# One core of attention: two instruction streams mixed by weights, with order edges between them added, other weights, and scales formed at other places

## The chip, the cores and the metric

The kernel runs on one core of a Trainium2 chip. The metric is the device time of one execution in microseconds. The engines are TensorE (PE; its weight loads, PEld, are listed apart), VectorE (DVE), ScalarE (ACT), GpSimd (POOL) and SyncE (SP), which issues nearly all DMA here. Each engine works through its own queue of instructions in the order in which the compiled program put them.

## What is computed

One inference step of a decoder of two layers, for a prompt of 2048 tokens and, beside it, 8 samples of 4 tokens each (1024 wide). Layer 0 has four heads of a gated linear recurrence (HGRN2) and four heads of forgetting attention; layer 1 is gated linear attention (GLA). The samples' attention reads its 2048 past keys and values from pages of a cache by a page table. The change touches the attention:

```python
def fox_prompt(q, k, v, log_f):                      # 16 blocks of 128 queries, 4 heads of 128
    c = jnp.cumsum(log_f, axis=1).swapaxes(1, 2)
    ...
    logits = einsum('bthd,bshd->bhts', qi, k) * scale + ci[..., None] - c[:, :, None, :]
    logits = jnp.where(t[:, None] >= key_pos[None, :], logits, -jnp.inf)
    p = jax.nn.softmax(logits, axis=-1)
    return einsum('bhts,bshd->bthd', p, v)

def fox_sample(q, k, v, log_f, k_pages, v_pages, logf_pages, page_table):   # 8 samples, 4 tokens
    k_past = k_pages[page_table].reshape(db, -1, H, dh)      # 16 pages of 128 rows a sample
    v_past = v_pages[page_table].reshape(db, -1, H, dh)
    ...
    p = jax.nn.softmax(concatenate([logit_past, logit_new], axis=-1), axis=-1)
    return einsum('bhts,bshd->bthd', p[..., :P], v_past) + einsum('bhts,bshd->bthd', p[..., P:], v)
```

The rest of a layer (the projections before, the output projection after) is matmul of 1024-wide weights.

## The kernel before, in words

The program has three phases: the projections of layer 0 with HGRN2 in two halves of 1024 tokens, then attention (`phase_fox`, from L1099), then the output of layer 0 and all of layer 1. Operands of matmuls that must be exact are held as two f16 parts (`h_*` and `l_*`, or `th` and `tl`), and `mm3` (L452 to L454) does three f16 matmuls for one product. To fit f16 the operands are scaled by powers of two; the scales are columns of one small tile `kc`, given out by `kcol` (L237).

**Two streams.** Attention is written as two Python generators, mixed by `mux` (L72). Each `yield` hands over a cost; `mux` takes the next piece of whichever stream has the smaller share of its total so far, and the totals are the constants `FOX_P` and `FOX_S`. The costs that the sample's stream hands over are constants too: `SC_C` for one head of one turn of keys, `PV_C` for one set of values. The mixing order is the order of tracing. A scheduler then places the instructions on each engine by it, by priority, and by extra edges: `issue_after(x)` says that what is traced inside stands behind `x` on the engine of `x`. Nothing of it is decided while the program runs; at run time engines only wait for data and for buffers.

**The prompt's stream** (`fox_prompt`, L1139) goes through 16 groups (head h, group G of 512 queries). `loads(h, G)` brings queries, keys, bias, values and the gate (`raw_q`, `raw_k`, `cb`, `raw_v`, `fsg`) by SyncE, and splits them: ACT writes `h_*`, POOL `l_*`; for values ACT first multiplies by the scale `self.sv`. It is called in the middle of the group before. `scores` makes one row of 128 queries: `s` on TensorE (`mm3`), the softmax on DVE, ACT and POOL (`mx`, `nm`, tiles `L`). `values` makes the output: TensorE transposes `L` to `pt` (L1217), ACT rounds `pt` to `th` (L1224), DVE takes the remainder `tl` (L1225), and `mm3` adds into `fo`.

**The sample's stream** (`fox_sample`, L1282) first goes through 32 turns of keys: four pages (`pgcache_fox_k`, 256 KB each) are fetched, TensorE transposes them into `pkt` (L1331), ACT and DVE copy them to `kts` (two copies each a turn, L1334 and L1335), and four `strips` of matmuls that lie side by side in the array add scores into `sc`. After turn 3 `past` sums the forget values of the cache. Then comes the softmax, and then the values: two accumulators `pv0` and `pv1`, each of 16 sets of four pages `pgcache_fox_v` and one set of new values; a set is four strips (L1465), one page each, with `high_priority`. Pages share one pool of `PG` = 27 buffers of 256 KB. SyncE issues every page (L1302) after it has loaded the page's number from the table into a register, four numbers at a time.

**Scales.** `y_bounds` (L1505), called at the start of `phase_fox`, forms bounds of the outputs of both layers, with three matmuls `spr_gh`, `spr_vm`, `spr_gg` (L248) that spread a maximum over the partitions and a chain of small DVE operations on single columns. It also forms `self.sv`, the scale of the prompt's values, from `vmax`, the measured maximum of the values (taken tile by tile in the projections). For queries and keys, `fox_scale` (L1487) does it from a bound that is known when the projection starts.

Of the kernel before, what the change touches and what calls it, by code (L numbers as in the profile page):

```python
# [8 lines left out]
F32 = mybir.dt.float32  # L9
# [6 lines left out]
ALU = mybir.AluOpType  # L16
# [3 lines left out]
P = 128  # L20
# [7 lines left out]
NPG = 16  # L28
# [5 lines left out]
S0 = 12000.0  # L34
SC_C = 700.0
Z_C = 4000.0
# [11 lines left out]
PG = 27  # L48
PAST = 12
NG = 2  # L50
WSPLIT = 4
FOX_S = 335000.0
FOX_P = 270000.0
# [5 lines left out]
DEC = 4500.0  # L59
PV_C = 4600.0  # L60
NEG = -1e30
# [41 lines left out]
class Kern:  # L103
# [6 lines left out]
    def consts(self):  # L110
        nc, i = self.nc, self.i
# [15 lines left out]

        self.kc, self.n_kc, self.scales = cp.tile([P, 176], F32, name="kc"), 0, {}
        self.vmax = cp.tile([P, NPG], F32, name="vmax")
# [107 lines left out]
    def kcol(self, n=1):  # L237
        self.n_kc += n
        assert self.n_kc <= 176
        return self.kc[:, self.n_kc - n : self.n_kc]  # L240
# [209 lines left out]
    def mm3(self, ps, lh, rh, first, last):  # L450
        nc = self.nc
        nc.tensor.matmul(ps, lh[0], rh[0], start=first, stop=False)  # L452
        nc.tensor.matmul(ps, lh[0], rh[1], start=False, stop=False)  # L453
        nc.tensor.matmul(ps, lh[1], rh[0], start=False, stop=last)  # L454

# [310 lines left out]
    def even_half(self, hf, act, wpool, wp, pps, npool, S):  # L766
# [94 lines left out]
        def mk_bkv(hp, which):  # L861
# [3 lines left out]
            def run(W):  # L865
                cs = slice(hp * 256, hp * 256 + 256)
                held = []
                if which == "k" and hf == 0:
                    self.fox_scale("k", hp)

# [65 lines left out]
    def phase_even(self):  # L936
# [4 lines left out]
        with pool("act", side="right") as ap, pool("w", side="right") as w0, pool("wl", side="right") as wp1, \  # L941
# [5 lines left out]
            nrm = Pool(n0, {"th": 1, "nss": 4, "rs_t": 4, "rs_r": 4})  # L947
            self.scales2, self.ready, self.fsc, self.logit = {}, {}, {}, {}
            self.sx_even = self.gain_scale(self.g_even, pps, "pj", "e")
# [155 lines left out]
    def phase_fox(self):  # L1105
        tc, nc = self.tc, self.nc
        with tc.tile_pool(name="fe", bufs=2, reuse_waits="tile") as f1, \
# [8 lines left out]
            nc.gpsimd.affine_select(caus, caus, [[-1, P]], ALU.is_ge, FAR, base=0, channel_multiplier=1)  # L1116
            self.y_bounds(pps)
            with tc.tile_pool(name="fs", bufs=1, side="right", reuse_waits="tile") as s0:
# [20 lines left out]
    def fox_prompt(self, fx, pps, caus):  # L1139
# [3 lines left out]
        self.turns = []  # L1143
        self.sample_done = False

# [6 lines left out]

        def loads(h, G):
            gs = slice(G * 512, (G + 1) * 512)
            Q[h, G] = self.load_split(fx, self.qTd[h][:, gs], f"q{h}{G}", "q")
            K[h, G] = self.load_split(fx, self.kTd[h][:, gs], f"k{h}{G}", "k")
            bias(h, G)
            vsrc = self.vd[gs, h * P : (h + 1) * P].rearrange("(c s) d -> s c d", s=P)
            V[h, G] = self.load_split(fx, vsrc, f"v{h}{G}", "v", self.sv[:, 0:1])
            SG[h, G] = fx.tile([P, 512], F32, tag="sg", name=f"fsg{h}{G}")  # L1160
            nc.sync.dma_start(SG[h, G], self.sgd[h][:, gs])

        def scores(h, G, b):
# [36 lines left out]
        def values(h, G, rows, po, b1, b2):  # L1200
# [29 lines left out]
            for j in range(nj):  # L1230
                if j + len(ahead) < nj:
                    ahead.append(turn(j + len(ahead)))
                th, tl, parts = ahead.pop(0)
                for s, a, c0 in parts:
                    vv = [x[:, (s % 4) * P : (s % 4 + 1) * P] for x in V[h, s // 4]]
                    self.mm3(po[:, c0:c2], vv, [x[:, a : a + c2 - c0] for x in (th, tl)], s == 0, s == ns - 1)
                yield sum(c2 - c0 for _, _, c0 in parts) * 2.1
            y = fx.tile([P, 512], F32, tag="y", name=f"fy{h}{G}{b1}")
            nc.vector.scalar_tensor_tensor(y[:, c1:c2], po[:, c1:c2], self.sv[:, 2:3], SG[h, G][:, c1:c2], ALU.mult,
                                           ALU.mult)  # L1240
# [23 lines left out]
    def strips(self, makers, sources):  # L1264


        with self.tc.high_priority():
# [4 lines left out]
            for m in makers[1:]:  # L1272
                m()

    def fox_sample(self, fs, pps):
# [29 lines left out]

        yield S0

        qs = one([P, NH, TS], "qs")
# [85 lines left out]
        for n in range(4 * DB + 1):  # L1394
            if n < 4 * DB:
# [57 lines left out]
        for g in range(2):  # L1453
            pv = pps.tile([P, 512], F32, tag="sc", name=f"pv{g}")
            for j in range(NPG + 1):
                makers, sources = [], []
                for bb in range(4):
# [5 lines left out]
                    else:  # L1463
# [23 lines left out]
    def fox_scale(self, which, hp):  # L1487


        nc = self.nc  # L1490
        c = self.scales[f"B{which}{hp}"][:, 2:3]
        up, down = self.fsc[which, hp] = self.kcol(), self.kcol()
        nc.vector.tensor_scalar(down, c, 2.0**19, 2.0**-20, ALU.mult, ALU.max)
        if which == "q":
            nc.vector.tensor_scalar(up, c, 2.0**20, 2.0**-19, ALU.mult, ALU.min)
            nc.vector.tensor_scalar(up, up, SCALE, None, ALU.mult)
            return
        nc.vector.reciprocal(up, down)

        ib, beta = self.logit[hp] = self.kcol(), self.kcol()  # L1500
# [3 lines left out]
    def y_bounds(self, pps):  # L1504
# [394 lines left out]
```

## Time and profile before

| | |
|---|---|
| median of 3 runs | 2440.97 us (2440.67 to 2441.5) |
| profiled execution, own time | 2450.02 us |
| its span | 2448.3 us, 54207 instructions |
| busy in the span | PE 2325.6 (95%), PEld 1652.6 (67%), DVE 1464.5 (60%), ACT 1131.8 (46%), POOL 746.5 (30%) |
| moved | 316.96 MB, mean 129 GB/s |
| pages of keys and of values | 128 and 128, 256.0 KB each, 3.9 and 3.7 us from issue to landing |

The profile is one execution, so its times are set against its own 2450.02 us, not against the median of the runs. Engine rows give busy time; what an engine waited for stands in brackets behind an instruction, or in the list of waits as "engine tile line <- releaser: us in total, times, longest". A busy TensorE may be running at a lower granted clock, which shows as a longer time of the same instruction. In the list of groups, f16 matmuls of the projections cost the most (L452 to L454, 282.5, 282.6 and 282.3 us for the output projection alone); of attention, the prompt's transposes L1217 take 89.5 us (x544), the page transposes L1331 78.3 us (x512). Attention is the 15th to 22nd of the page's forty slices, where the DMA moves 199 to 255 GB/s.

### The profile page before, as it was taken

The numbers are of one execution on the slowest core, as the hardware profiler recorded it, in microseconds if no ns is written. First come the engines' busy times: TensorE is split into PE (matmuls) and PEld (weight loads), VectorE is DVE, ScalarE is ACT, GpSimd is POOL, SyncE is SP. The second block draws the span as 40 slices with busy tenths as digits, with TensorE's granted clock in tenths as the row PEclk, the third lists the DMA queues.
The fourth block names the chain that finished last, engine by engine and source line by source line (L and its number), as shares of the span: only waits on it lengthen the run. The fifth ranks groups of instructions, "written<-read, shape, count | busy, mean of one in ns | idle before, by whom it ended". The sixth has DMA issues, their size and how long they took to land. (4 is left out here: it accounts for less than half of the span.)

```text
span 2448.3 us, 54207 instructions
## 1 busy us (share of the span) xinstructions
PE 2325.6 (95%) x21116; PEld 1652.6 (67%) x21116; DVE 1464.5 (60%) x3337; ACT 1131.8 (46%) x2465; POOL 746.5 (30%) x825
## 2 busy tenths in 40 slices
PE   7999999999999989999788999999999999998998
PEld 5667668855655865666345786777768766666887
DVE  7656657446765637667556353665675555557564
ACT  6433343343433137666456454545542645545243
POOL 2223323012213235533333320332443222322233
PEclk9999999999999989999999999999999999999999
DMA  6222235435431277666684631222246312114454
GB/s 178 77 80 70 75 105 170 142 106 147 140 114 58 89 233 232 222 199 202 217 255 134 214 107 44 62 74 75 66 140 191 116 45 62 43 57 151 141 194 151
DMA packets 297955, 316.96 MB, mean 129 GB/s; under 512 B 39729, under 2 KB 241010, under 8 KB 297698
## 3 DMA queue, kind: packets, MB, share of 16 engines
q1 hardware_dynamic: 295234, 308.98, 40.0%
q8 instruction: 166, 2.72, 0.5%
q10 hardware_dynamic: 2160, 3.93, 0.4%
q14 instruction: 91, 0.75, 0.1%
q0 software_dynamic: 304, 0.59, 0.1%
HBM read 242.31 MB, written 71.11 MB: 128 GB/s over the span
## 5 line engine op out<-in xcount | busy, mean ns | idle before, releaser
L452 PE MATMUL pt_o<-w_o,act 128*128 128x256 f16 x1024 | 282.5, 276 | 2.7 <-ACT w_o L334 1.4
L453 PE MATMUL pt_o<-w_o,act 128*128 128x256 f16 x1024 | 282.6, 276 | 0.9 <-POOL w_o L335 0.9
L454 PE MATMUL pt_o<-w_o,act 128*128 128x256 f16 x1024 | 282.3, 276 | 0.0
L452 PEld LDWEIGHTS <-act 128*128 128x128 f16 (+1 forms) x2320 | 228.6, 99 | 40.8 <-issue 10.0
L453 PEld LDWEIGHTS <-act 128*128 128x128 f16 (+1 forms) x2320 | 228.5, 98 | 33.7 <-issue 3.2
L454 PEld LDWEIGHTS <-act 128*128 128x128 f16 (+1 forms) x2320 | 228.6, 99 | 33.3 <-issue 4.1
L623 POOL TENSOR_TENSOR kA<-kA,fA 128x512 f32<-128x512 f32 (+1 forms) x56 | 80.6, 1438 | 203.2 <-PE gl_A L595 124.0
L454 PE MATMUL pt_Cv<-w_Cv,act 128*128 128x256 f16 (+1 forms) x520 | 142.5, 275 | 0.0
L452 PE MATMUL pt_Cv<-w_Cv,act 128*128 128x256 f16 (+1 forms) x520 | 142.3, 275 | 0.0
L453 PE MATMUL pt_Cv<-w_Cv,act 128*128 128x256 f16 (+1 forms) x520 | 142.0, 275 | 0.0
L1189 ACT ACTIVATE L<-L,nm,kc 128x512 f32<-128x512 f32 (+3 forms) x160 | 118.2, 741 | 32.6 <-DVE nm L1187 30.3
L623 POOL TENSOR_TENSOR kC<-kC,fC 128x512 f32<-128x512 f32 (+1 forms) x56 | 81.9, 1463 | 164.5 <-PE gl_C L595 76.8
L1197 POOL TENSOR_SCALAR L<-L,nm 128x512 f32<-128x512 f32 (+3 forms) x160 | 97.9, 627 | 101.0 <-DVE nm L1193 29.8
L1225 DVE TENSOR_TENSOR tl<-pt,th 128x512 f16<-128x512 f32 (+3 forms) x159 | 95.5, 609 | 47.1 <-ACT th L1224 45.9
L1224 ACT ACTIVATE th<-pt 128x512 f16<-128x512 f32 (+3 forms) x159 | 82.1, 527 | 84.6 <-PE pt L1217 78.6
L1217 PE MATMUL pt<-ident,L 128*128 128x128 f32 x544 | 89.5, 278 | 0.2 <-POOL L L1197 0.2
L1331 PEld LDWEIGHTS pkt<-ident,pgcache_fox_k 128*128 128x128 f32 x512 | 60.6, 144 | 42.3 <-issue 25.9
L1331 PE MATMUL pkt<-ident,pgcache_fox_k 128*128 128x128 f32 x512 | 78.3, 282 | 7.9 <-DMA pgcache_fox_k<-in_cache_fox_k 4.9
L1217 PEld LDWEIGHTS pt<-ident,L 128*128 128x128 f32 x544 | 68.8, 144 | 23.0 <-issue 2.0
L452 PE MATMUL pt_Bv<-w_Bv,act 128*128 128x256 f16 (+2 forms) x264 | 72.3, 274 | 0.0
L454 PE MATMUL pt_Bv<-w_Bv,act 128*128 128x256 f16 (+2 forms) x264 | 72.2, 274 | 0.0
L453 PE MATMUL pt_Bv<-w_Bv,act 128*128 128x256 f16 (+2 forms) x264 | 72.2, 274 | 0.0
(1086 smaller groups left out, 6882.8 us busy)
## 6 DMA issues: line engine op xcount, KB each, us to landing
pgcache_fox_k<-in_cache_fox_k SPq DMA_DIRECT2D x128, 256.0 KB, 3.9
pgcache_fox_v<-in_cache_fox_v SPq DMA_DIRECT2D x128, 256.0 KB, 3.7
yr<-yT SPq DMA_DIRECT2D x16, 1024.0 KB, 5.7
nx<-in_x_prompt SPq DMA_DIRECT2D x16, 512.0 KB, 5.7
wr_Aqf<-in_w_in_even SPq DMA_DIRECT2D x64, 128.0 KB, 2.7
wr_o<-in_w_out_even SPq DMA_DIRECT2D x32, 256.0 KB, 5.2
wr_Cv<-in_w_in_odd SPq DMA_DIRECT2D x32, 256.0 KB, 3.5
wr_Cqk<-in_w_in_odd SPq DMA_DIRECT2D x64, 128.0 KB, 2.7
```

Of the source, the lines that this page charges most:

```text
L452: nc.tensor.matmul(ps, lh[0], rh[0], start=first, stop=False)
L453: nc.tensor.matmul(ps, lh[0], rh[1], start=False, stop=False)
L454: nc.tensor.matmul(ps, lh[1], rh[0], start=False, stop=last)
L623: nc.gpsimd.tensor_tensor(kv[:, :, 0], kv[:, :, 0], t1.to_broadcast([P, nb, w]), ALU.mult)
L1189: nc.scalar.activation(lt[:, :w], lt[:, :w], AF.Exp, bias=nm[:, 0:1], scale=ib, accum_out=nm[:, 2 + j : 3 + j])
L1197: nc.gpsimd.tensor_scalar(lt[:, :w], lt[:, :w], nm[:, 1:2], 2.0**14, ALU.mult, ALU.mult)
L1217: nc.tensor.transpose(pt[:, w : w + P], rows[b][s // 4][0][:, (s % 4) * P : (s % 4 + 1) * P], self.ident)
L1224: nc.scalar.activation(th[:, a:w], pt[:, a:w], AF.Copy),
L1225: nc.vector.tensor_tensor(tl[:, a:w], pt[:, a:w], th[:, a:w], ALU.subtract)))
L1331: nc.tensor.transpose(pk[:, j * P : (j + 1) * P], pgs[j][:, h * P : (h + 1) * P], self.ident)
```

## The change

1. *Order.* The prompt's stream keeps in `last_pe` its last matmul (`mm3` now returns it). Before each set of value strips that matmul is put into `marks`, and the strips stand behind the one of the set before (`VAHEAD` = 2: the last but one entry, counting the new one). So a set of strips cannot be placed further forward on TensorE than the point that the prompt's tracing had reached a set earlier.
2. *Loads of a prompt group* are placed behind `last_s`: the last copy of a key turn (ACT or DVE), or the last strip of a set. The edge binds what the loads put on that instruction's own engine.
3. *Weights.* `SC_C` 700 to 800, `PV_C` 4600 to 5860, `FOX_S` 335000 to 411000. `FOX_P` stays at 270000.
4. *The values' scale* comes from `fox_scale("v", hp)`, a bound for each pair of heads formed when the projection starts, with its inverse in `v_undo`; `self.sv` goes.
5. *Output bounds.* `y_bounds` is called in the sample's stream after `past`, not at the start of attention. `kc` grows from 176 to 184 columns.

```diff
-SC_C = 700.0
+SC_C = 800.0
+VAHEAD = 2
-FOX_S = 335000.0
+FOX_S = 411000.0
-PV_C = 4600.0
+PV_C = 5860.0
...
@@ mm3
-        nc.tensor.matmul(ps, lh[1], rh[0], start=False, stop=last)
+        return nc.tensor.matmul(ps, lh[1], rh[0], start=False, stop=last)
@@ mk_bkv
-                if which == "k" and hf == 0:
-                    self.fox_scale("k", hp)
+                if hf == 0:
+                    self.fox_scale(which, hp)
@@ phase_fox
-            self.y_bounds(pps)
@@ fox_prompt
         def loads(h, G):
+            with ExitStack() as st:
+                if self.last_s is not None:
+                    st.enter_context(self.tc.issue_after(self.last_s.ins))
+                fetch(h, G)
+
+        def fetch(h, G):
...
-            V[h, G] = self.load_split(fx, vsrc, f"v{h}{G}", "v", self.sv[:, 0:1])
+            V[h, G] = self.load_split(fx, vsrc, f"v{h}{G}", "v", self.fsc["v", h // 2][0])
...
-                self.mm3(ps[:, :w], q, [x[:, :w] for x in K[h, j]], True, True)
+                self.last_pe = self.mm3(ps[:, :w], q, [x[:, :w] for x in K[h, j]], True, True)
...                                   # (in values the same: self.last_pe = self.mm3(po..., )
@@ strips
             for m in makers[1:]:
-                m()
+                self.last_s = m()
@@ fox_sample
+        marks = []
...
                     new.append(turn(c, b, h, pgs))
+                    self.last_s = new[-1][1]
                     yield SC_C
...
                 yield from past()
+                self.y_bounds(pps)
...
-                self.strips(makers, sources)
+                marks.append(self.last_pe)
+                with self.tc.issue_after(marks[max(0, len(marks) - VAHEAD)].ins):
+                    self.strips(makers, sources)
                 yield PV_C
@@ fox_scale
         nc.vector.reciprocal(up, down)
+        if which == "v":
+            self.v_undo[hp] = self.kcol()
+            nc.vector.tensor_scalar(self.v_undo[hp], down, 2.0**-15, None, ALU.mult)
+            return
@@ y_bounds
-        vm, self.sv = self.spread(self.vmax[:, :NPG], pps, "kt", "vm"), self.kcol(3)
-        nc.vector.tensor_scalar(f, f, vm, 0.5, ALU.mult, ALU.mult)
-        self.power2(vm, 2.0**14, self.sv)
-        nc.vector.tensor_scalar(self.sv[:, 2:3], self.sv[:, 1:2], 2.0**-15, None, ALU.mult)
+        nc.vector.tensor_scalar(f, f, self.spread(self.vmax[:, :NPG], pps, "kt", "vm"), 0.5, ALU.mult, ALU.mult)
```

What it makes of the order is shown at three places. First TensorE in the value stretch, where the sets of pages 7 and 8 of the first four samples stand. `pgcache_fox_v07` is page 7 of sample 0, `pv0` the accumulator; `fo`, `s` and `pt` belong to the prompt. Before:

```order
L1465 MATMUL pv0_14928<-pgcache_fox_v07_15705,pT1_14870 16x512
L1465 MATMUL pv0_14928<-pgcache_fox_v17_15707,pT1_14870 16x512
L1465 MATMUL pv0_14928<-pgcache_fox_v27_15709,pT1_14870 16x512
L1465 MATMUL pv0_14928<-pgcache_fox_v37_15711,pT1_14870 16x512
L1448 MATMUL pptn_14922<-ident_58,pr_10844 32x128
L1465 MATMUL pv0_14928<-pgcache_fox_v08_15844,pT2_14871 16x512
L1465 MATMUL pv0_14928<-pgcache_fox_v18_15846,pT2_14871 16x512
L1465 MATMUL pv0_14928<-pgcache_fox_v28_15848,pT2_14871 16x512
L1465 MATMUL pv0_14928<-pgcache_fox_v38_15850,pT2_14871 16x512
```

And after, in the same place:

```order
L1476 MATMUL pv0_14768<-pgcache_fox_v07_15608,pT1_14716 16x512
L1476 MATMUL pv0_14768<-pgcache_fox_v17_15610,pT1_14716 16x512
L1476 MATMUL pv0_14768<-pgcache_fox_v27_15612,pT1_14716 16x512
L1476 MATMUL pv0_14768<-pgcache_fox_v37_15614,pT1_14716 16x512
L1224 MATMUL pt1305_15523<-ident_58,L1121_14713 128x128
L1459 MATMUL pptn_14762<-ident_58,pr_10786 32x128
L1224 MATMUL pt1305_15523<-ident_58,L1131_14966 128x128
L1224 MATMUL pt1305_15523<-ident_58,L1141_15091 128x128
L1224 MATMUL pt1305_15523<-ident_58,L1151_15215 128x128
L453 LDWEIGHTS h_q20_14838
L453 MATMUL s230_15735<-h_k20_14844,h_q20_14838 128x512
```

Before, the next set stands behind one transpose; after, 71 rows of the prompt's work stand between the two sets. The first set of values moved forward on TensorE too, from row 12237 to row 11836.

Second ACT in the key stretch, at the loads of the prompt's group (1, 2) (`h_q12`, `h_k12`, `raw_v12` are its splits, `kts260` the copy of strip 2, sample 6, head 0, so of the 23rd turn of keys, `th` the prompt's rounding). Before, the splits stand one by one among the prompt's work:

```order
L1334 ACTIVATE kts122_12231<-pkt122_12226 128x512
L1189 ACTIVATE L110_12800,nm11_12803<-L110_12800,nm11_12803,kc_67 128x256
L1224 ACTIVATE th0304_12723<-pt0304_12718 128x512
L1135 ACTIVATE h_q12_13413<-raw_q12_13411 128x512
L1189 ACTIVATE L120_12975,nm12_13030<-L120_12975,nm12_13030,kc_67 128x384
L1334 ACTIVATE kts130_12306<-pkt130_12301 128x512
L1135 ACTIVATE h_v11_12575<-raw_v11_12573 128x512
```

After, they stand together behind the last copy of the 24th turn, `kts272`:

```order
L1343 ACTIVATE kts262_13519<-pkt262_13514 128x512
L1343 ACTIVATE kts270_13591<-pkt270_13586 128x512
L1343 ACTIVATE kts272_13621<-pkt272_13616 128x512
L1135 ACTIVATE h_q12_13639<-raw_q12_13637 128x512
L1135 ACTIVATE h_k12_13645<-raw_k12_13643 128x512
L1134 ACTIVATE raw_v12_13650<-raw_v12_13650,kc_67 128x512
L1135 ACTIVATE h_q13_14066<-raw_q13_14064 128x512
```

The key copies themselves stand earlier against the prompt: `h_q12` is beside the 11th and 12th turn before, behind the 24th after.

Third TensorE at the start of attention (`spr_*` are the spreading matmuls of `y_bounds`, `s000` the first scores). Before:

```order
L248 MATMUL spr_gh_10510<-ident_58,kc_67 128x128
L452 LDWEIGHTS h_q00_10546
L452 MATMUL s000_10570<-h_k00_10552,h_q00_10546 128x128
L453 LDWEIGHTS h_q00_10546
L453 MATMUL s000_10570<-l_k00_10553,h_q00_10546 128x128
```

After, the scores stand first, and `spr_gh` comes 367 rows further on, among the first turns of keys:

```order
L453 LDWEIGHTS h_q00_10518
L453 MATMUL s000_10542<-h_k00_10524,h_q00_10518 128x128
L454 LDWEIGHTS h_q00_10518
L454 MATMUL s000_10542<-l_k00_10525,h_q00_10518 128x128
L455 LDWEIGHTS l_q00_10519
L455 MATMUL s000_10542<-h_k00_10524,l_q00_10519 128x128
```

The lines below L452 are one further on in the kernel after, and those of attention seven to eleven.

More of the change, by code (lines that the diff above doesn't have):

```diff
@@ L126, in consts @@
         self.g_even = col("g_even", i["norm_even"][0], KT)
-        self.kc, self.n_kc, self.scales = cp.tile([P, 176], F32, name="kc"), 0, {}
+        self.kc, self.n_kc, self.scales = cp.tile([P, 184], F32, name="kc"), 0, {}
         self.vmax = cp.tile([P, NPG], F32, name="vmax")
@@ L238, in kcol @@
         self.n_kc += n
-        assert self.n_kc <= 176
+        assert self.n_kc <= 184
         return self.kc[:, self.n_kc - n : self.n_kc]
@@ L947, in phase_even @@
             nrm = Pool(n0, {"th": 1, "nss": 4, "rs_t": 4, "rs_r": 4})
-            self.scales2, self.ready, self.fsc, self.logit = {}, {}, {}, {}
+            self.scales2, self.ready, self.fsc, self.logit, self.v_undo = {}, {}, {}, {}, {}
             self.sx_even = self.gain_scale(self.g_even, pps, "pj", "e")
@@ L1143, in fox_prompt @@
         self.turns = []
-        self.sample_done = False
+        self.sample_done, self.last_s = False, None
         def bias(h, g):
@@ L1235, in values @@
                     vv = [x[:, (s % 4) * P : (s % 4 + 1) * P] for x in V[h, s // 4]]
-                    self.mm3(po[:, c0:c2], vv, [x[:, a : a + c2 - c0] for x in (th, tl)], s == 0, s == ns - 1)
+                    self.last_pe = self.mm3(po[:, c0:c2], vv, [x[:, a : a + c2 - c0] for x in (th, tl)], s == 0,
+                                            s == ns - 1)
                 yield sum(c2 - c0 for _, _, c0 in parts) * 2.1
             y = fx.tile([P, 512], F32, tag="y", name=f"fy{h}{G}{b1}")
-            nc.vector.scalar_tensor_tensor(y[:, c1:c2], po[:, c1:c2], self.sv[:, 2:3], SG[h, G][:, c1:c2], ALU.mult,
+            nc.vector.scalar_tensor_tensor(y[:, c1:c2], po[:, c1:c2], self.v_undo[h // 2], SG[h, G][:, c1:c2], ALU.mult,
                                            ALU.mult)
```

## The prediction

> **What bounds the kernel now.** I read the page first, then busy time by windows of the attention stage, then the waits of TensorE there, then TensorE's and SyncE's timelines where the waits are.
>
> The first rows are the windows (stretch, its us, busy us with instructions of each engine, granted clock, DMA share, GB/s). The stage runs from the first scores (893) to the last matmul into `fo` (1341.5).
>
> ```profile
> core 0: us, PE busy (x) PEld busy (x) DVE busy (x) ACT busy (x) POOL busy (x), PEclk, DMA share, GB/s
> 905.00:1174.00 269.00, 258.47 (x1861) 164.34 (x1865) 194.97 (x588) 183.23 (x415) 125.21 (x201) 0.97 0.65 212
> 1174.00:1290.00 116.00, 93.76 (x622) 41.98 (x614) 61.73 (x202) 52.59 (x121) 41.02 (x65) 0.99 0.79 255
> 1290.00:1342.00 52.00, 42.97 (x293) 30.10 (x290) 36.30 (x100) 34.65 (x75) 19.40 (x30) 0.93 0.38 116
> ```
>
> TensorE is the bound while the cached keys are transposed (905 to 1174: 258 of 269 us) and falls to 94 of 116 us while the cached values are multiplied. DVE, ACT and POOL are no fuller there, so it waits for something else. Its waits, for 1174 to 1300, for 900 to 1174 and for the rest:
>
> ```profile
> PE pv L1465 <- DMA pgcache_fox_v<-in_cache_fox_v: 20.3, 19, 3.1
> PE pv L1465 <- DVE oS L1471: 1.7, 1, 1.7
> PE fo L452 <- ACT th L1224: 0.9, 1, 0.9
> PE oT L1474 <- DVE oS L1471: 0.6, 1, 0.6
> ```
> ```profile
> PE fo L452 <- ACT th L1224: 3.6, 3, 2.4
> PE pkt L1331 <- ACT kts L1334: 2.2, 1, 2.2
> ```
> ```profile
> PE fo L452 <- ACT th L1224: 3.4, 2, 3.3
> PE fo L453 <- DVE tl L1225: 2.8, 8, 0.5
> ```
>
> So 20.3 us, 19 waits, are for pages of values. Is that the transfer, or its issue? SyncE's timeline in that stretch, with the landing times of the pages:
>
> ```profile
> 1218.27 32.78 SPq L1302 DMA_DIRECT2D pgcache_fox_v<-in_cache_fox_v  x32
> 1251.16 0.37 SPq L1130 DMA_DIRECT2D raw_q<-qTd  x1
> 1251.64 0.37 SPq L1130 DMA_DIRECT2D raw_k<-kTd  x1
> ```
> ```profile
> DMA to landing us min/median/max: 2.5/3.7/6.1
> ```
>
> From 1218.27 to 1251.16 SyncE issues 32 pages in one unbroken run: 32.9 / 8 = 4.11 us for a set of four (loading their numbers from the table counts in it). A page lands 3.7 us after its issue and is used at once. So the issue is the bound: one set in 4.11 us, however many of the 27 page buffers are free.
>
> How often does TensorE ask? From its timeline in the value stretch:
>
> ```profile
> 1186.38 0.60 PE L1217 MATMUL pt<-ident,L 128*128 128x128 f32 x4
> 1186.82 0.38 PE L452 MATMUL fo<-th,h_v 128*128 128x512 f16 x1
> 1187.04 0.38 PE L453 MATMUL fo<-tl,h_v 128*128 128x512 f16 x1
> ...
> 1188.17 1.05 PE L1465 MATMUL pv<-pgcache_fox_v,pT 128*16 128x512 f32 x8
> 1189.15 0.39 PE L452 MATMUL fo<-th,h_v 128*128 128x512 f16 x1
> ```
>
> From start to start four 128-wide fp32 transposes take 0.44 us, a 512-column f16 matmul 0.22, a set of four strips (8 passes) 0.98. With these pitches (0.109 us a transpose, 0.42 ns an f16 column) I added up the rows of the order before. From the first to the last page set there stand 97,408 f16 columns (41 us), 145 transposes (16) and 33 sets (32): 89 us. The first ten sets stand 0, 1.0, 2.0, 3.0, 4.0, 4.9, 6.4, 8.4, 9.5 and 12.7 us of work after the first, the later ones about 3.2 apart. 27 pages (6.75 sets) lie ready, the 28th page is issued when the first strip has run, and from there a set comes every 4.11 us and lands 3.7 later: set 8 at 8.1 (in time), set 9 at 12.2 (2.7 late), and about 0.9 more is lost on each of the next 22: some 22 us, where the trace has 20.3. So the two numbers explain the waits.
>
> **The change, part by part.**
>
> *Value strips no further forward than the prompt.* The order now has 184,704 f16 columns (78 us), 251 transposes (27) and 33 sets (32) between first and last value set: 137 us for the same pages. What came before shrinks (keys 223 to 188 us, the softmax between 14 to 11), and so does the prompt alone at the end (37 to 27): the sum, 362.5 us, is the same. Sets 7 to 13 are wanted at 6.4, 9.5, 17.3, 23.3, 29.1, 30.1 and 31.1; by 27 buffers and 4.11 us they have landed at 4.0, 8.1, 12.2, 16.3, 20.4, 24.5 and 28.6. After that sets are wanted every 5 us on average, so SyncE gains ground even with five loads of a prompt group (0.5 us each, 1251.16 to 1251.64) between. The 20.3 falls to about 2, and the waits for `oS` (1.7 + 0.6) mostly stay out, as 9 us of prompt now stand before the second accumulator's first set. I take 22.6 - 2 = 20.6 off; bounds 12 (queue held up by a prompt load) and 22.6.
>
> *Clock.* What follows the two longest waits for pages:
>
> ```profile
> 1223.67 1.05 PE L1465 MATMUL pv<-pgcache_fox_v,pT 128*16 128x512 f32 x8 [2.91 <-DMA pgcache_fox_v<-in_cache_fox_v]
> 1224.65 0.50 PE L452 MATMUL fo<-th,h_v 128*128 128x512 f16 x1
> 1224.95 0.63 PE L453 MATMUL fo<-tl,h_v 128*128 128x512 f16 x1
> ...
> 1227.51 0.63 PE L454 MATMUL fo<-th,l_v 128*128 128x512 f16 x1
> ...
> 1256.84 1.05 PE L1465 MATMUL pv<-pgcache_fox_v,pT 128*16 128x512 f32 x8 [3.09 <-DMA pgcache_fox_v<-in_cache_fox_v]
> 1257.82 0.39 PE L452 MATMUL s<-h_k,h_q 128*128 128x512 f16 x1
> ```
>
> After a wait of 2.9 us the matmuls took 0.63 us instead of 0.38 from 1224.6 to 1228, for 3.4 us; after one of 3.1 they did not. I take half of 3.4 us, 1.7, as gone with the wait; bounds 0 (a new wait does the same elsewhere) and 3.4 (two). The Trainium skill, TensorE: Matmul & The Clock Gate, section HAM oscillation, has the rule that only idle gaps over about 3.4 us cost the clock; by it no wait here, at most 3.1 long, does, and this term would be 0. The trace differs, at one wait of two.
>
> *Output bounds out of the stage's start.* About 30 tiny DVE operations and three matmuls stood before and among the first scores; the waits there:
>
> ```profile
> 894.93 0.49 PE L248 MATMUL spr_vm<-ident,kc 128*128 128x128 f32 x2 [1.18 <-DVE kc L246]
> 898.98 0.48 PE L452 MATMUL s<-h_k,h_q 128*128 128x384 f16 x1 [3.34 <-DVE mx L1181]
> 904.97 0.69 PE L1331 MATMUL pkt<-ident,pgcache_fox_k 128*128 128x128 f32 x2 [4.87 <-DMA pgcache_fox_k<-in_cache_fox_k]
> ```
>
> The first two (4.5 us) go, but the next instruction of TensorE is still the first key page, which lands at 904.9 and is issued behind the same loads: its wait grows by what they lose. I take 0.5 for scores that are ready sooner; bounds 0 and 1.2. Put among prompt scores later, the same operations cost TensorE three matmuls; their DVE chain has other work around it: 0. The values' scale from a bound adds some five one-column DVE operations for each pair of heads in the projections, where TensorE does not wait for them: 0. The larger column tile: 0.
>
> *Keys packed denser.* From the 17th key turn to the last the order has 6.6 us of TensorE work a turn before and 5.0 after, some as little as 2.7. Each turn needs two copies on ACT and two on DVE:
>
> ```profile
> L1334 ACT ACTIVATE kts<-pkt x64: 570/592/601, 909.3 to 1155.3; 128x512 f32<-128x512 f32 x64
> L1335 DVE COPY kts<-pkt x64: 672/691/698, 909.5 to 1156.0; 128x512 f32<-128x512 f32 x64
> ```
>
> And the loads of a prompt group are now queued on ACT behind the sample's last copy: in the order `h_q12` and `h_k12` stand right behind `kts272`, and the scores that read them only 0.9 us of work behind its transposes; `h_q11` has 2.3 us. What such a queue costs, before shows at its one dense place: ACT waits 2.89 us in front of a prompt load, a key copy stands behind it, and TensorE waits 2.15 us for that.
>
> ```profile
> 1099.91 0.72 ACT L1134 ACTIVATE raw_v<-raw_v,kc 128x512 f32<-128x512 f32 x1 [2.89 <-DVE smx L1418]
> 1100.54 0.58 ACT L1334 ACTIVATE kts<-pkt 128x512 f32<-128x512 f32 x1
> ...
> 1101.17 0.66 PE L1331 MATMUL pkt<-ident,pgcache_fox_k 128*128 128x128 f32 x4 [2.15 <-ACT kts L1334]
> ```
>
> I count two to three more such waits, +5; bounds 0 and 16 turns x 1.5 = 24 (nearest to the first: the rest of that stretch had none). Key pages have room: SyncE waited for TensorE to free buffers there, not the reverse,
>
> ```profile
> SPq L1302 <- PE pkt L1331: 67.4, 45, 5.4
> ```
>
> and 5.0 us a turn is still more than 4.11. In exchange for the waiting of the ACT loads nothing else is late: the page leads of six turns stay.
>
> *More prompt beside the values, less alone.* Beside the values stand 104 us of prompt work instead of 57. The prompt's own waits were 3.6 us in the 269 us above: +2, bounds 0 and 4. Alone at the end it waited 3.4 + 2.8 us over 37 us; with 27 left, -1.5, bounds 0 and -2.
>
> *Sum.* -20.6 - 1.7 - 0.5 + 5 + 2 - 1.5 = -17.3. The profiled execution took 2450.0 us, 1.7 more than its span and 9 more than the median of the runs, 2441.0. So 2432.7 profiled, and 2423.7 as a median. All at the good end is -29 (2412).
>
> **Rivals.**
>
> A, the pages wait anyway. SyncE's waits from 1150 to 1180 (us in total, times, the longest):
>
> ```profile
> SPq L1302 <- PE pv L1465: 9.7, 6, 8.3
> ```
>
> If the loads that now stand among the pages in SyncE's queue (`fsg20` needs `fo12`, `raw_q30` a buffer) hold the queue once or twice for 8 us or so, as the longest of these waits, the lead of 27 pages is gone and two thirds of the waits stay, 14; with the other terms the gain is 17.3 - 12 = 5: 2436, and with the clock term lost 2438. For it: just before the values SyncE did stand still that long, a page waiting for a buffer. Against: every load there waits for work that TensorE has behind it when the queue arrives.
>
> B, slower: copies become the bound. If each of the last 16 dense key turns costs the 2.15 us of the one dense place, with its two operand places the same, that is 18 x 2.15 = 38.7 instead of 5: -17.3 + 33.7 = +16.4, 2457. It decides above 1.2 us a turn (22.3 / 18). For it: the two PSUM buffers and the row above. Against: ACT 183 and DVE 195 of 269 us busy leave room, and four copies in 5.0 us take 1.3 on each.
>
> C, the holding does nothing, because what is traced last is often no ACT instruction: the order shows otherwise at both places.
>
> **Chances.** Forecast 0.73 (2412 to 2436; three quarters of it between 2418 and 2430), A 0.14 (half below 2436), B 0.10, a rest of 0.03 as now. The range 2412 to 2441 holds the forecast and A and leaves out B. About 0.2%, 4.9 us, is what can be told from no change: faster 0.78, same 0.10, slower 0.12.
>
> **What would show it.** Right: waits of `pv` for pages under 5 us in all; SyncE waiting for `pv` to free buffers in the value stretch; that stretch about 145 us and the end alone about 40; waits of `pkt` for `kts` of some 5 us more. Wrong: `pv` still waiting over 10 us with SyncE never idle (A), or TensorE's waits for `kts` and for `h_q` or `l_q` above 20 us (B).

## The result: 0.7% slower

The kernel after takes 2460.16 us (2456.81 to 2466.74, 4 runs) against 2441.23 of before: a ratio of 1.0073, 95% interval 1.0057 to 1.0089. That is 18.9 us more, where 17.3 less were forecast. The profiled execution took 2466.74 us, span 2465.0. The last matmul into `fo` now ends at 1354.9 us where it was 1341.5, so most of the time went inside the attention stage. Its windows (stretch, its us, busy us of each engine, granted clock, DMA share, GB/s) are keys, softmax between, values, prompt alone, first before, then after:

```profile
904.97:1155.21 250.24, 240.78 (x1717) 154.33 (x1718) 180.22 (x540) 170.78 (x389) 119.27 (x192) 0.97 0.67 220
1155.21:1172.94 17.73, 16.66 (x134) 9.68 (x133) 14.31 (x47) 11.76 (x24) 5.39 (x9) 1.00 0.32 104
1172.94:1290.60 117.66, 95.42 (x638) 42.47 (x638) 62.17 (x204) 53.31 (x125) 42.20 (x66) 0.99 0.78 251
1290.60:1340.87 50.27, 42.14 (x288) 29.87 (x281) 35.76 (x98) 33.66 (x73) 17.70 (x28) 0.93 0.36 112
```
```profile
904.40:1120.20 215.80, 204.00 (x1495) 129.35 (x1496) 148.12 (x442) 134.27 (x299) 86.76 (x144) 0.99 0.72 232
1120.20:1140.20 20.00, 15.19 (x122) 9.83 (x119) 13.21 (x43) 13.27 (x29) 11.94 (x15) 0.83 0.60 185
1140.20:1316.80 176.60, 151.48 (x949) 74.34 (x948) 106.59 (x360) 98.11 (x230) 73.44 (x114) 0.93 0.60 189
1316.80:1354.90 38.10, 31.24 (x215) 23.40 (x215) 27.84 (x74) 26.18 (x57) 14.77 (x21) 0.91 0.43 136
```

The keys shrank and the prompt alone shrank as the order had said. But the value stretch takes 176.6 us for 137 us of work, at a clock of 0.93 (before: 117.7 for 89, at 0.99). Set against the work that the order gives each stretch, the values lost about 11 us, 3 of them as idle time of TensorE and the rest as longer busy time at the lower clock; the softmax between lost 5, the keys 1, and the end gained 2. What TensorE waits for beside the values, from 1140 to 1317 (us in total, times, longest):

```profile
PE fo L453 <- ACT th L1231: 17.7, 7, 9.0
PE pt L1224 <- POOL L L1204: 4.0, 1, 4.0
PE fo L454 <- DVE tl L1232: 1.8, 6, 0.4
```

The 20.3 us of waits for pages are gone, as forecast. In their place stand 23.5 us of waits for the prompt's own operands. The longest, on TensorE's timeline:

```profile
1184.03 0.27 PE L453 MATMUL fo<-th,h_v 128*128 128x128 f16 x1 [9.02 <-ACT th L1231]
1184.08 0.63 PE L453 MATMUL s<-h_k,h_q 128*128 128x512 f16 x1
...
1187.47 0.38 PE L455 MATMUL s<-h_k,l_q 128*128 128x512 f16 x1
```

`th` is a rounding by ACT that takes half a microsecond. ACT's timeline says why it was late: in front of it in ACT's queue stands the split of a load of the prompt, `h_k` of head 3, and that load had not come.

```profile
1172.92 0.19 ACT L1196 ACTIVATION_READ_ACCUMULATOR L<-L,nm,kc 128x1 f32 x1
1182.35 0.63 ACT L1135 ACTIVATE h_k<-raw_k 128x512 f16<-128x512 f32 x1 [9.24 <-DMA raw_k<-kTd]
1183.09 0.72 ACT L1134 ACTIVATE raw_v<-raw_v,kc 128x512 f32<-128x512 f32 x1
1183.72 0.75 ACT L1231 ACTIVATE th<-pt 128x128 f16<-128x128 f32 x2
```

And SyncE's timeline says why the load had not come:

```profile
1135.84 0.32 SPq L1130 DMA_DIRECT2D raw_q<-qTd  x1
1141.31 36.33 SPq L1310 DMA_DIRECT2D pgcache_fox_v<-in_cache_fox_v  x37
1178.06 0.34 SPq L1130 DMA_DIRECT2D raw_k<-kTd  x1
1178.51 0.38 SPq L1128 DMA_DIRECT2D raw_v<-vd  x1
```

Between `raw_q30` and `raw_k30` lie 42 us, 36.3 of them a run of 37 pages. (The expectations below count 40 there, and three too many for the other orders.) The chain is: pages on SyncE, behind them a load, behind that a split on ACT, behind that `th`, behind that TensorE. And SyncE in turn waits in the value stretch for TensorE to free page buffers, so the queue waits also for what it holds up (of this sum, under 4 us fall inside the run of 37):

```profile
SPq L1310 <- PE pv L1476: 35.8, 19, 9.0
```

The waits cost twice. After the 9 us, TensorE runs at half clock for 3.5 us, and its clock is low after shorter ones too (after one of 2.39 us, and after one of 4.04 with one of 2.80 behind it):

```profile
1184.00:1187.50 3.50, 3.47 (x14) 2.06 (x14) 3.12 (x11) 2.08 (x5) 1.69 (x3) 0.51 0.77 234
1200.90:1206.00 5.10, 5.10 (x25) 1.33 (x25) 3.06 (x11) 3.40 (x8) 1.57 (x2) 0.67 0.84 265
1249.50:1256.00 6.50, 6.30 (x23) 2.48 (x23) 2.27 (x5) 1.09 (x3) 0.00 (x0) 0.52 0.27 84
```

### The profile page after: what moved, and what is told of

Its sections match the earlier page's. It is cut to its first block, busy times and chain, and to the rows that moved or that the text cites. A ratio compares the mean times of both kernels' runs of the same rounds, so it can differ in the third digit from the quotient of the medians.

```text
span 2465.0 us, 54252 instructions
## 1 busy us (share of the span) xinstructions
PE 2331.1 (95%) x21116; PEld 1653.4 (67%) x21116; DVE 1465.1 (59%) x3339; ACT 1134.1 (46%) x2465; POOL 747.7 (30%) x825
## 5 line engine op out<-in xcount | busy, mean ns | idle before, releaser
L453 PE MATMUL fo<-th,h_v 128*128 128x512 f16 (+3 forms) x174 | 59.7, 343 | 25.0 <-ACT th L1231 24.7
L453 PE MATMUL pt_Bv<-w_Bv,act 128*128 128x256 f16 (+2 forms) x264 | 72.2, 273 | 0.0
L455 PE MATMUL pt_Bv<-w_Bv,act 128*128 128x256 f16 (+2 forms) x264 | 72.2, 273 | 0.0
```

Source lines behind the costliest of these rows:

```text
L455: return nc.tensor.matmul(ps, lh[1], rh[0], start=False, stop=last)
```

## The experiments

Theory Q: the loads of the prompt stand behind pages on SyncE, and the roundings behind the loads on ACT. Its rival W: the prompt's chain of scores, softmax and rounding cannot keep up with so much work beside the values, whoever issues what. Every ratio is to before, with its 95% interval.

### Which edit it is

**Parts 4 and 5 alone** (`scales_only`: weights and both kinds of edges as before).

```diff
-SC_C = 800.0
-FOX_S = 411000.0
-PV_C = 5860.0
+SC_C = 700.0
+FOX_S = 335000.0
+PV_C = 4600.0
-                if self.last_s is not None:
+                if False:
-                with self.tc.issue_after(marks[max(0, len(marks) - VAHEAD)].ins):
-                    self.strips(makers, sources)
+                self.strips(makers, sources)
```

> The kernel before with parts 4 and 5 of the change alone: the values' scale from a bound, the output bounds formed after the summing of the forget values. All theories: no change that can be told, 2439 to 2443; the first scores come some 4 us sooner and the first key page is waited for that much longer. Were the time 5 us or more above before, the two scales would be a cause of their own.

2441.65 us, 0.9994 (0.9984 to 1.0005). The scales are no cause. At the start TensorE waits 8.3 us for the first key page in place of 4.9, as the prediction had it: what the scores gain, the page takes back.

**Without the edge on the loads** (`no_loadedge`).

```diff
-                if self.last_s is not None:
+                if False:
```

> The kernel after without the edge that holds a prompt group's loads behind the sample's last copy; value strips are still held, weights as after. In the order the loads of head 3 stand among the first sets of pages again, as before the change, keys take 219 us of TensorE's work and values 95. Theory Q: no wait of ACT for a load in the value stretch, but 33 sets at 4.11 us on SyncE outlast 95 us of work again: waits for pages return, about 15 to 20 us, and the time is near before, 2436 to 2444. Rival W: with less of the prompt beside the values the waits for th go too, and nothing else comes: below 2434.

2441.08 us, 0.9994 (0.9984 to 1.0004): all of the 18.9 us go with this one edge. TensorE's waits in the value stretch are again those of before, somewhat fewer (13.4 us for pages, where Q had said 15 to 20):

```profile
PE pv L1476 <- DMA pgcache_fox_v<-in_cache_fox_v: 13.4, 10, 3.3
PE oT L1488 <- DVE oS L1485: 1.5, 1, 1.5
PE fo L453 <- ACT th L1231: 1.4, 2, 0.7
```

The order also settles what the prediction had put down to the wrong edit. Counting transposes, f16 columns and strips alone, the keys have 215 us of TensorE's work before and 181 after, the values 88 and 136. Without the edge on the loads it is 219 and 95; without the holding of the strips 181 and 89. It is the loads' edge that moves 35 us of prompt work out of the key stretch. The holding of the strips only decides whether that work stands beside the values or behind them.

**Without the holding of the value strips** (`no_vahead`).

```diff
-                with self.tc.issue_after(marks[max(0, len(marks) - VAHEAD)].ins):
-                    self.strips(makers, sources)
+                self.strips(makers, sources)
```

> The kernel after without the holding of the value strips; the edge on the loads and the weights as after. In the order values have 89 us of work, the prompt alone at the end 73 (before: 37), and raw_k30 again stands behind 40 pages. Theory Q: both prices are paid, waits for pages of some 20 us and waits for th behind late loads of some 10 to 15: 2460 to 2475. Rival W: with less of the prompt beside the values the waits for th go away and only those for pages stay: 2440 to 2450.

2459.39 us, 1.0064 (1.0051 to 1.0077). The time is just under what Q said, and the mechanism is not Q's: no waits for `th` in the value stretch, only the old ones for pages, although `raw_k30` is issued 40 us after `raw_q30` here too.

```profile
PE pv L1476 <- DMA pgcache_fox_v<-in_cache_fox_v: 19.8, 12, 3.1
PE pv L1476 <- DVE oS L1484: 1.3, 1, 1.3
```

Most of the loss is in the prompt alone at the end, whose 73 us of work take 96 (before: 37 in 50):

```profile
1258.00:1354.00 96.00, 82.99 (x519) 54.91 (x516) 73.26 (x228) 67.74 (x154) 43.00 (x66) 0.93 0.25 74
```

So with these weights the loads' edge costs 17 to 19 us whether the work that it moves stands beside the values or behind them; waits behind late loads are seen only in the first case. Why the work behind the values costs some 10 us more than its share, no run here settles.

### Is it the queue?

**The prompt's loads issued by ACT** (`loads_actq`), and **the same loads ahead by priority** (`loads_first`), each one edit to the kernel after:

```diff
-            nc.sync.dma_start(r, src)          # loads_actq; likewise for the values' form
+            nc.scalar.dma_start(r, src)
...
+        with self.tc.high_priority():          # loads_first
+            nc.sync.dma_start(r, src)
```

> The kernel after, with the prompt's loads of queries, keys and values issued by ACT itself, not by SyncE. Theory Q (queue): in the kernel after, raw_k30 stands behind 40 pages of values on SyncE, comes 42 us after raw_q30, and ACT waits for it with the roundings th queued behind. Here no load stands behind a page: TensorE's 9.0 us wait for th goes, its waits for th in the value stretch fall from 17.7 us to under 6, and the time from 2460 to 2440 to 2447. Rival W (chain): TensorE waits for th because the prompt's softmax cannot keep up beside the values, whoever issues the loads: waits for th stay above 12 us there, and the time at 2455 to 2462.

> The kernel after, with a higher priority for SyncE's loads of the prompt's queries, keys and values: in SyncE's order raw_k30 then stands behind 24 pages of the run in place of 40, so some 16 us sooner (a page takes 1.03 us to issue). Theory Q: the 9.0 us wait for th goes, the shorter ones (2.4, 4.0, 2.8) only in part, 2448 to 2454. Rival W: no change beyond 4 us from the kernel after's 2460.

`loads_actq` 2449.42 us, 1.0027 (1.0018 to 1.0036); `loads_first` 2448.07, 1.0018 (1.001 to 1.0027): 11 and 12 us of the 18.9 come back. Waits for `th` in the value stretch, of the one and of the other:

```profile
PE fo L453 <- ACT th L1231: 8.3, 5, 3.2
```
```profile
PE fo L453 <- ACT th L1232: 7.9, 6, 3.7
```

The 9 us wait is gone in both, but they gain in different places. By the profiles, the value stretch of `loads_actq` takes 165.2 us at a clock of 0.98, where after has 176.0 at 0.93: all of its gain. That of `loads_first` is as long as after's (175.8 us, 962 matmuls for 946); its gain stands in the keys (212.3 us for 215.8) and the softmax (14.9 for 20.1). So it is `loads_actq` that shows what the queue costs beside the values.

Q had said under 6 us and at most 2447 for it, so a part stays. Not all of that part is W's: ACT stood 5 us in front of its own issue of a load, the wait ended with a page, and behind it came the longest of TensorE's waits for `th`, 3.2 us.

```profile
1182.10 0.36 ACTq L1130 DMA_DIRECT2D raw_k<-kTd  x1
1182.51 0.55 ACT L1231 ACTIVATE th<-pt 128x256 f16<-128x256 f32 x2 [5.06 <-DMA pgcache_fox_v<-in_cache_fox_v]
```

In the compiled order this load, `raw_k32`, waits for page `pgcache_fox_v50`, by a link that the part on SyncE's issue below explains. So a load was moved to ACT's queue and still hung on a page.

**The old weights with the new edges** (`old_weights`: the three constants as in `scales_only`).

> The kernel after with the weights of before (SC_C 700, PV_C 4600, FOX_S 335000); both kinds of edges stay. In the order values have 126 us of work beside them (after: 136), and raw_k30 stands with raw_q30 ahead of the page run, not 40 pages behind. Theory Q: no 9 us wait for th, 2443 to 2451. Rival W (the chain cannot keep up beside the values): 2453 to 2460, in proportion to the work beside the values. Other loads (raw_v31, raw_q32) still stand behind pages there, so the lower end is not expected of either.

2448.18 us, 1.0024 (1.0011 to 1.0037). The time fits Q, yet the 9 us wait is there, for another load: `raw_v` of group (3, 1), 45 pages behind the `raw_k` of its group (runs of 28, 5 and the 12 shown). SyncE, ACT and TensorE:

```profile
1182.68 10.87 SPq L1310 DMA_DIRECT2D pgcache_fox_v<-in_cache_fox_v  x12
1193.65 0.38 SPq L1128 DMA_DIRECT2D raw_v<-vd  x1
```
```profile
1198.37 0.72 ACT L1134 ACTIVATE raw_v<-raw_v,kc 128x512 f32<-128x512 f32 x1 [10.64 <-DMA raw_v<-vd]
1198.99 0.74 ACT L1231 ACTIVATE th<-pt 128x128 f16<-128x128 f32 x2
```
```profile
1199.30 0.27 PE L453 MATMUL fo<-th,h_v 128*128 128x128 f16 x1 [9.24 <-ACT th L1231]
1199.36 0.63 PE L453 MATMUL s<-h_k,h_q 128*128 128x512 f16 x1
```

So the mechanism of Q is there, but its forecast that the wait goes is not met, and the time was right by luck: TensorE waits 18.6 us for `th` in this value stretch, more than after's 17.7, and the kernel is 12 us faster than after all the same. Part of that lies elsewhere: by the profiles the end takes 31.2 us at a clock of 1.00, where after has 38.3 at 0.91. The sum of these waits alone does not set the time. The new weights without either edge were not run.

### Is SyncE's issue the bound?

A page costs SyncE 1.03 us with its share of loading the numbers and of asserting that each lies in the pool. Three kernels leave that out (before, after and `no_loadedge` with it), with one edit:

```diff
-                        vals, (mybir.EngineType.SP,), min_val=0, max_val=n_pool - 1)
+                        vals, (mybir.EngineType.SP,), min_val=0, max_val=n_pool - 1,
+                        skip_runtime_bounds_check_because="page numbers are a permutation of the pool")
```

> The kernel before, without the check on SyncE that a page's number lies in the pool (the assertions and their register operations go; of a set's 4.1 us before, 0.93 is loading four numbers, 4 x 0.26 their handling and check, 4 x 0.55 the pages). Theory I (the waits for pages before are SyncE's issue): a set takes 3.2 to 3.7 us, TensorE's waits for pages fall from 20.3 to under 10 us, and the time by about 10, to 2430 to 2437. Rival D (the transfer itself limits, 256 KB landing in 3.7 us): the waits stay above 15 us and the time at 2438 to 2443. The order has 80 us of work beside the values and 43 in the prompt alone behind them, 7 us the worse way round in both.

> The kernel after, without the check of the page numbers on SyncE. In its order raw_k30 stands behind 35 pages in place of 40, and each takes some 0.8 us in place of 1.03, so it comes some 13 us sooner. Theory Q: the 9.0 us wait for th goes and the time falls by 8 to 15 us, to 2446 to 2452. Rival W: waits for th and L in the value stretch stay above 18 us, 2456 to 2460.

> The kernel after without the edge on the prompt's loads, as no_loadedge, and without the check of the page numbers on SyncE. In the order values have 98 us of work, the prompt alone behind them 26, and head 3's loads stand among the first sets. Theory Q with I: 33 sets at 3.2 to 3.7 us fit the stretch but for 0 to 10 us, no wait for th comes in their place: 2425 to 2434, faster than both kernels. Rival W (the chain takes over as the pages stop limiting): waits for th and L in the value stretch rise from 2 to over 10 us, 2436 to 2442.

A page now costs 0.80 us, 3.2 us a set (`noedge_short_issue`, 27 pages of one run):

```profile
1190.49 21.70 SPq L1311 DMA_DIRECT2D pgcache_fox_v<-in_cache_fox_v  x27
```

`after_short_issue` is 2443.27 us, 1.0001 (0.999 to 1.0012), 17 us less than after: nearly the whole loss, more than Q had said, from a shorter time on SyncE. But by the profiles only 5 us of that stand in the value stretch (171.1 us for 176.0; the longest wait for `th` is 6.0 in place of 9.0), 6 in the keys and 5 in the softmax, so it is not the price of the late loads alone. In `before_short_issue` the waits for pages fall to 2.6 us, which speaks for SyncE's issue, not the transfer, as their cause (a new wait also gives pages time there; `before_short_pool` below has 4.9 us without it). But it takes 2439.83 us, 0.9984 (0.9972 to 0.9997), and `noedge_short_issue` 2439.44, 0.9993 (0.9983 to 1.0004), both much slower than theory I said and in the range of the rivals. A new wait of 8.5 to 8.9 us for `th` has taken the place of those for pages, and no load is late here. ACT in `noedge_short_issue`:

```profile
1213.03 0.19 ACT L1196 ACTIVATION_READ_ACCUMULATOR L<-L,nm,kc 128x1 f32 x1
1223.47 0.33 ACTq L1249 DMA_DIRECT2D yT<-fy  x1
1223.90 1.08 ACT L1231 ACTIVATE th<-pt 128x512 f16<-128x512 f32 x2 [10.68 <-DMA pgcache_fox_v<-in_cache_fox_v]
```

The profile puts the wait to `th` and a page, which `th` does not read. What waited is the store of the prompt's output in front of it, whose `fy` was ready at 1213.8. The compiled order shows the link: DMAs of SyncE and ACT take turns on eight completion semaphores (counters that tell that a transfer has landed), and each waits until the one before it on the same semaphore has landed. For this store that is page `pgcache_fox_v74`, which SyncE issued only at 1218.85; the store left at 1223.47.

```
SP   L1311 DMA pgcache_fox_v74_15723<-in_cache_fox_v 128x512 [waits DMAHW7_49,PE_49]
ACT  L1249 DMA yT0_76<-fy220_15590 128x512 [waits DMAHW7_49,DVE_49]
ACT  L1231 ACTIVATE th2300_15635<-pt2300_15630 128x512 [waits PE_49,Activation_49]
```

### Taking the stores off ACT

`noedge_short_pool` is `noedge_short_issue`, and `before_short_pool` is `before_short_issue`, each with

```diff
-            (nc.scalar if c2 - c1 == 512 else nc.gpsimd).dma_start(self.yT[0][NH + h]...
+            nc.gpsimd.dma_start(self.yT[0][NH + h]...
```

> As noedge_short_issue, with the prompt's outputs (fy into yT) stored by POOL's queue in place of ACT's. In noedge_short_issue ACT stood 10.7 us until 1223.5 in front of such a store although fy was ready at 1213.8; the wait ended with a page of values, which SyncE issues. Theory L (the store waits for a page whose completion signal it shares, and the roundings th are queued behind it): the 8.5 us wait of TensorE for th goes, with the slow clock behind it: 2426 to 2434. Rival (the wait is the prompt's own chain): the same wait stays, 2436 to 2441.

> The kernel before without the check of the page numbers on SyncE, and with the prompt's outputs stored by POOL's queue; nothing of the change. Theory L: the 8.9 us wait for th of before_short_issue goes, 2427 to 2434. It is 0 to 5 us slower than noedge_short_pool, whose prompt has 26 us alone at the end in place of 43. Rival: 2437 to 2441.

2421.49 us, 0.9921 (0.9904 to 0.9938), and 2431.74, 0.9962 (0.9946 to 0.9979). Theory L holds: the wait is gone in both, and the first of the two beats before by 21 us (19 by the ratio) and after by 39. It is faster than L had said (2426 to 2434), and the 10 us between the two are more than the 0 to 5 expected. What TensorE waits for in its value stretch (114 us for 98 of work):

```profile
PE pv L1477 <- DMA pgcache_fox_v<-in_cache_fox_v: 4.3, 4, 1.8
PE pt L1224 <- DVE tl L1232: 2.5, 2, 2.3
PE pv L1477 <- DVE oS L1486: 1.5, 1, 1.5
```

`before_short_pool` waits 4.9 us for pages and takes as long for values and end together. The two windows of `before_short_pool`, then of `noedge_short_pool`:

```profile
1170.70:1263.50 92.80, 86.78 (x591) 36.88 (x594) 53.72 (x182) 47.72 (x114) 41.27 (x65) 0.98 0.91 312
1263.50:1323.80 60.30, 49.95 (x333) 33.90 (x326) 43.68 (x122) 38.83 (x85) 22.37 (x35) 0.97 0.33 104
```
```profile
1162.70:1276.80 114.10, 105.23 (x706) 48.79 (x705) 70.79 (x229) 59.36 (x142) 48.34 (x77) 0.99 0.78 263
1276.80:1315.80 39.00, 32.09 (x222) 23.61 (x215) 27.90 (x74) 26.88 (x58) 15.32 (x22) 0.91 0.42 134
```

Both come to 153.1 us; before it was 168.6 (1172.9 to 1341.5). So here the holding of the strips shifts prompt work from behind the values to beside them and gains nothing by it. (In `no_loadedge` the two stretches are 5 us shorter than before's by the profile; the median shows no gain.) Between the two profiled executions lie 6.6 us, and the key stretch has 7.6 (251.1 and 243.5 us): TensorE waits there 5.4 us for `kts` and 2.8 for `mx`, against 0.8 and 0.6. Which edit does that, stays open.

### What the edge costs once nothing hangs on the pages

`after_loads_pool` is the kernel after, with the prompt's loads and the stores on POOL's queue and without the assertions.

```diff
-            nc.sync.dma_start(r, src)          # likewise for the values' form
+            nc.gpsimd.dma_start(r, src)
```

> The kernel after, all edges and weights kept, with the prompt's loads of queries, keys and values and the stores of its outputs on POOL's queue, and without the check of the page numbers on SyncE. In the order 140 us of work stand beside the values, 26 in the prompt alone. Compared with noedge_short_pool (2421.5) it tells what the edge on the loads still costs once no load and no store hangs on the pages. Theory Q alone (the edge costs only by that queue): idle time of TensorE beside the values under 12 us, 2419 to 2428. Rival W (the prompt's chain cannot keep up with 140 us beside the values): over 15 us idle there, most of it for th, L and mx, 2432 to 2445.

2435.29 us, 0.9966 (0.995 to 0.9981): inside W's range. In the value stretch TensorE is idle for 169.7 - 153.5 = 16.2 us, at a clock of 0.97:

```profile
1123.10:1292.80 169.70, 153.47 (x978) 75.85 (x977) 111.33 (x380) 104.17 (x246) 95.91 (x150) 0.97 0.63 210
```
```profile
PE pt L1224 <- POOL L L1204: 5.1, 1, 5.1
PE fo L453 <- ACT th L1231: 3.9, 4, 1.5
PE fo L454 <- DVE tl L1232: 3.8, 13, 0.5
```

So both theories hold, for a part each. Of the 39 us between after and `noedge_short_pool`, 25 go with the queues of loads and stores and SyncE's shorter issue together, and 14 stay with the edge (by the ratios, 26 and 11). TensorE's idle time beside the values is 16.2 us with 140 us of work there, at a clock of 0.97, and 8.9 with 98, at 0.99; with 140 it waits for the prompt's chain, in many small pieces. How much of these 14 comes from POOL, which now issues DMAs as well and is the releaser of the longest wait, stays open.

## Why the prediction was wrong

**Pages of values, -20.6: right.** 20.3 us became 0, and SyncE waited for `pv` instead of `pv` for SyncE. The reason given, issue at 4.11 us a set, was shown by leaving work out of the issue (4.9 us in `before_short_pool`).

**More prompt beside the values, +2 (bounds 0 and 4): this is the step that failed.** It measured 23.5 us, so TensorE's idle time beside the values did not fall with the waits for pages (25 us after, 22 before), and with the clock the stretch lost 11 us against its work where the three terms for it (-20.6, -1.7, +2) had promised 20.3 less. The +2 came from the rate of such waits in the key stretch, where the prompt's loads had come long before. I had seen that loads stand among the pages, and asked only one way round: whether a load holds up the pages (rival A). The other, a page run that holds up a load, and ACT in order behind it, was not asked. The order had the answer: `raw_k30` 37 pages behind `raw_q30`, 38 us at the 1.03 us that the trace gave, while its split on ACT stood in front of a `th` wanted at once. Taking the loads off that queue (`loads_actq`) made the stretch 10.8 us shorter. The sentence that SyncE "gains ground" was true, and was the trouble: it gains ground by running through pages first.

**Clock, -1.7: wrong sign.** The value stretch went from 0.99 to 0.93. The three slow runs of matmuls shown above alone lose 3.5 x 0.49 + 5.1 x 0.33 + 6.5 x 0.48 = 6.5 us. About as much idle time as before came in fewer, longer pieces: waits of 9.0, of 2.4 and of 4.0 with 2.8 us were each followed by a low clock (0.51, 0.67, 0.52), where in before one wait for a page of nineteen was. The Trainium skill, TensorE: Matmul & The Clock Gate, section HAM oscillation, puts the price on idle gaps over about 3.4 us; the 9.0 and the 4.0 us wait agree with it, the 2.39 us one, with 5.1 us at 0.67 behind it, does not.

**Keys denser, +5: about right.** Waits of `pkt` for `kts` rose from 2.2 to 6.3 us, and rival B's price did not come; the whole stretch lost 1 us against its work. (B's sum takes 18 turns where its text has 16; with 16 it would be 2453, not 2457.)

**Softmax between keys and values: not in the sum.** It lost 5 us against its work, with waits of 2.9 us for `th` and 1.9 for `L` and a clock of 0.83. `loads_actq` leaves it at 20.0 us, `loads_first` and `after_short_issue` have 14.9 and 14.6. The cause stays open.

**Start, -0.5, and the end, -1.5: right.** The end's idle time fell by 1.4 us, and the first key page's wait grew to 8.6.

**Which edit moves the work: wrong.** The 137 us beside the values need both edges; the holding of the strips alone gives 95. The forecast time did not hang on it, but the part that I called harmless in exchange, loads waiting on ACT, is the edit without which the loss is gone. And the 20.6 us were not all to be had: `before_short_pool`, which leaves only 4.9 us of the waits for pages and moves little else, gains 11 us as a median (9 by the ratio), 15.5 in values and end by its profile.

Against after's 18.9 us the profiles give 13.4 us in the stage (its end, 1354.9 for 1341.5); the rest lies within what single executions of either kernel differ by (2440.67 to 2450.02 for before).

## What to carry to other kernels

When a queue is freed to run ahead, list what stands behind it that others wait for, not only what it waits for itself: here a run of 37 prefetches cost as much as the late prefetches had. Follow every in-order link to its end, from the issuing queue over the engine that first touches the data to what is queued behind that. In this kernel prefetches with many buffers and loads with few did better on separate issuing queues, and a store did better off an engine whose next instruction is on the critical path. Moving a DMA to another queue does not by itself free it: look for semaphores that the queues share.

## What the runs showed of the hardware

Issue of a page by a number from a table cost SyncE 1.03 us, against 3.7 us from issue to landing, and 0.80 without the range assertion. The Trainium skill, DMA: Bandwidth & Descriptors, section Issuing engines are not separate DMA queues, says that issuing from several engines saves only the time to initiate, usually small beside the transfer; here the issue was the bound beside the values. Moving the stores to POOL was worth 8 and 18 us, and moving the loads to ACT 11, by what no longer stood behind a page.

A store of ACT stood 10 us (1213.8 to 1223.5) until a page of SyncE had landed, by way of a shared completion semaphore; the profile showed it only as a wait of the next instruction for a tile that it does not read.
